# Weight block sums of a seven-product matrix scheme: from VectorE subtractions to adding transfers

## The chip, the cores and the metric

The kernel runs on one core of a Trainium2 chip. A core has five engines that run side by side and wait for one another through semaphores: TensorE (PE: matrix products, with a second stream, PEld, that loads the stationary operand), VectorE (DVE: elementwise work), ScalarE (ACT: functions, copies and casts), GpSimd (POOL) and SyncE (SP, which here only issues transfers). Sixteen transfer (DMA) engines move data between the chip's main memory and the core's on-chip memory; transfers can be issued from SP's queue, from ACT's or from GpSimd's. PE writes its products into eight banks of a separate accumulation memory.

The metric is the device time of one execution, in microseconds (us), the median of several runs. A profile is one further execution, recorded by the hardware.

## The reference

A decoder of two layers over 512 tokens of width 1024. Each layer is a feed-forward block, a mixing block (three kinds of attention with gates), and a second feed-forward block, each between two RMS norms. All values are float32. The change touches the four feed-forward blocks alone:

```python
D_MODEL, SEQ, DEPTH = 1024, 512, 2
D_FF = 2816                       # 22 tiles of 128

def _swiglu(t, w_gate, w_up, w_down):
    return (jax.nn.silu(t @ w_gate) * (t @ w_up)) @ w_down
...
for l in range(DEPTH):
    f = _swiglu(_rmsnorm(h, ffn1_pre_g[l]), ffn1_w_gate[l], ffn1_w_up[l], ffn1_w_down[l])
    h = h + 0.5 * _rmsnorm(f, ffn1_post_g[l])
    ...
    f = _swiglu(_rmsnorm(h, ffn2_pre_g[l]), ffn2_w_gate[l], ffn2_w_up[l], ffn2_w_down[l])
    h = h + 0.5 * _rmsnorm(f, ffn2_post_g[l])
```

## The kernel before

**Precision.** Every operand of a product is split into a high part (a cast to the format that PE multiplies) and a low part (the rest). A product is then three matmuls (`mm3`, L214 to L216): high by high, high by low, low by high. `split` (L185) makes the two parts: a cast on ACT (L188, or L191 with a scale) and a subtraction on DVE (L189 or L192).

**Seven products instead of eight.** The feed-forward's matrix products are cut into 2 x 2 blocks and computed with seven block products, numbered 0 to 6, in the manner of Strassen and Winograd. Four of the products need sums or differences of weight blocks, and four need sums of blocks of the other factor. One *set* of seven block products is one run through the scheme. Each feed-forward block has six sets: four *column groups* of the gate and up projection (`group`, with `gate_up` as the product; tile names with `t`, as in `pta`, `raw_ta`, `kta`, `wh_ta`), whose left block column is the gate weight and whose right block column is the up weight, and two halves of the down projection (`products`, with `product`; names with `d`, as in `pda`, `raw_da`, `bta`). The letter at the end, a or c, is the first or the second feed-forward block of a layer. The rest of the hidden width goes through ordinary products (`halved`, `gates`, `ups`, `down`), which lie between the sets.

**Units.** A block of weights has four tiles of 128 rows and is loaded as two *units* of two tiles (128 x 1024 elements, 512 KB). `BlockUnit` (L288 on) is such a unit. Its `fetch` issues transfers: into a raw buffer (tag `raw`, a ring of four buffers) or into a *kept* tile (`Keep`, L358; `kt` tiles of the tag `v` in a column group, `bt` tiles of the tag `k` in a down half). Its `load` forms the block that the product needs and splits it into `wh` and `wl` (four buffers each). With (row, column) for a block of the weights, the raw transfers and sums were:

- product 0: block (0,0), raw; product 1: block (1,0), raw
- product 2: t = (0,1) - (0,0): the first into kept tile 0, the second raw; one subtraction (L337)
- product 3: t = (1,1) - t: (1,1) into kept tile 1; one subtraction (L340)
- product 4: (1,1) from kept tile 1
- product 5: (1,1) - (0,1): the second raw; one subtraction in place (L345)
- product 6: t with (1,0), raw; one subtraction in place (L349)

The column groups run the products in the order 0, 2, 3, 4, 5, 1, 6 (`ORDER`), but the first group of a block in the order 0 to 6 (`FIRST`); the down halves run in `ORDER`.

**Order of the work.** `Queue` holds a list of jobs, each with the units it needs. When a job begins, its own units are loaded and then those of the jobs after it until four units are ahead (`load_ahead`, `AHEAD = 4`). After each load `fetch_ahead` walks along the list and fetches what isn't fetched yet; it stops at the first unit that needs a ring buffer when all four are taken. A compiler behind this text assigns the buffers and all semaphores and orders each engine's instructions by priority and estimated times, except where `tc.keep_in_program_order` pins one to its place in the text (the transfers into kept tiles are pinned). All weight transfers before the change are issued by SP (L262, L313). GpSimd has some small work at the beginning and in the mixing blocks (L123, L124: two small vector loads that PE transposes at L127; L1174, L1445 to L1447, L1249 to L1251) and none in the feed-forward sets.

Of the kernel before, what the change touches and what calls it, by code (L numbers as in the profile page):

```python
# [12 lines left out]
AF = mybir.ActivationFunctionType  # L13
ALU = mybir.AluOpType
# [3 lines left out]
P = 128  # L18
# [4 lines left out]
def kernel(  # L23
# [38 lines left out]
    nc = tc.nc  # L62
# [225 lines left out]
    class BlockUnit(Unit):  # L288
# [4 lines left out]

        BLOCKS = ((0, 0), (1, 0), (0, 0), None, None, (0, 1), (1, 0))

        def __init__(self, n, src, rows, k0, nk, ncol, keep, name, pair=None):
# [3 lines left out]
            self.pair = pair  # L302

        def waits(self):
            return not self.fetched

        def ring(self):
            return self.BLOCKS[self.n] is not None

        def block(self, dst, b):  # L310
            r = (b[0] * self.rows + self.k0) * P
            src, c = (self.src, b[1] * self.ncol) if self.pair is None else (self.pair[b[1]], self.c0)
            return nc.sync.dma_start(dst, src[r:r + self.nk * P, c:c + self.ncol].rearrange("(k p) c -> p k c", p=P))  # L313

        def fetch(self):
            if self.fetched:
                return
            self.fetched = True
            if self.n == 2:
                tc.keep_in_program_order(self.block(self.keep.get(0, self.k0), (0, 1)))  # L320
            if self.n == 3:
                tc.keep_in_program_order(self.block(self.keep.get(1, self.k0), (1, 1)))
            if self.ring():
                Q.fetched += 1
                self.raw = stile([P, self.nk, self.ncol], "raw", "raw_" + self.name, F32)
                self.block(self.raw[:], self.BLOCKS[self.n])

        def load(self):
            if self.h is not None:
                return  # L330
            self.fetch()
            t = self.keep.get(0, self.k0) if self.n >= 2 else None
            b = self.keep.get(1, self.k0) if self.n >= 3 else None
            if self.n < 2:
                src = self.raw[:]
            elif self.n == 2:
                nc.vector.tensor_tensor(t, t, self.raw[:], ALU.subtract)  # L337
                src = t
            elif self.n == 3:
                nc.vector.tensor_tensor(t, b, t, ALU.subtract)  # L340
                src = t
            elif self.n == 4:
                src = b
            elif self.n == 5:
                nc.vector.tensor_tensor(b, b, self.raw[:], ALU.subtract)  # L345
                src = b
            else:
                ins = (t, self.raw[:]) if self.pair is None else (self.raw[:], t)
                nc.vector.tensor_tensor(t, *ins, ALU.subtract)  # L349
                src = t  # L350
            self.split_from(src)
            if self.ring():
                self.raw = None
                Q.fetched -= 1
            Q.fetch_ahead()
# [288 lines left out]
    def ffn(l, src, wg, wu, wd, dst, name, spare, aside=None):  # L644
# [45 lines left out]
        def parts_of(n):  # L690
            r, tag = st["a", n]
            t = stile([P, 2, 4, S // 2], tag, f"ag{name}_{n}")
            split(t[:, 0], t[:, 1], r)
            st["ag", n] = t

        def sums():

            whole(1, 0)
            whole(1, 1)
            block_sum(2, 11, 10, 11, ALU.add, "k")  # L700
# [4 lines left out]
            block_sum(3, 0, 11, 0, ALU.subtract, "k")  # L705
            parts_of(3)
            yield
            whole(0, 1)
            block_sum(4, 1, 1, 0, ALU.subtract, "tri")
            parts_of(4)  # L710
            parts_of(5)
            yield
# [17 lines left out]
        def gate_up(f, n, uns, last_of_top):  # L730
            seeded = ("gb", 1) in st if n == 1 else False
            if n in (0, 1, 2) and not seeded:
                st["gb", SUM[n]] = [pbank("mm", f"pt{name}_{f}_{n}_{e}") for e in range(2)]
            pts = st.pop(("gb", 1)) if n == 1 else st["gb", SUM[n]]
            opens, ends = n in (0, 1, 2), n in (1, 4, 6)
            for un in uns:
                for k in range(un.nk):
                    kk = un.k0 + k
                    for e in range(2):
                        mm3(pts[e][:], *input_block(n, kk, e), un.h[:, k], un.l[:, k], opens and kk == 0 and not seeded,  # L740
                            ends and kk == ND // 2 - 1, free=True)
# [12 lines left out]
            if n == 1 and not seeded:  # L754
                nc.scalar.activation(t[:], t[:], AF.Silu)
            if n == 4 and last_of_top == 1:
                st["gb", 1] = seeds("mm", f"pt{name}_{f}_1", [st["c", 0, 0][:, e] for e in range(2)])
            if n == 6 or n == last_of_top:
                u = st["c", i, 1]
                nc.vector.tensor_tensor(u[:], u[:], st["c", i, 0][:], ALU.mult)  # L760
                st["hid", f, i] = u

        def feature_major(f):

            for i in range(2):
                u = st.pop(("hid", f, i))
                for b in range(2):
# [7 lines left out]
                    out_ = pt[:].rearrange("p (m q) -> p m q", m=2)  # L775
                    nc.scalar.copy(pair(f2)[:, :, HALVES[i]], out_)

        def group(f):

            order = FIRST if f == TG[0] else ORDER  # L780
            top = max((1, 4), key=order.index)
            keep = Keep(lambda i, k0: stile([P, 2, S], "v", f"kt{name}_{f}_{i}_{k0}", F32)[:])
            for n in order:
                uns = []
                for k in range(0, ND // 2, 2):
                    uns.append(BlockUnit(n, wg[l], ND // 2, k, 2, S, keep, f"t{name}_{f}_{n}_{k}", (wg[l], wu[l])))
                    uns[-1].c0 = f * P
# [56 lines left out]
        def first_factor(ci, n):  # L844

            nm = f"{name}_{ci}_{n}"
            h, l = (stile([P, FC // 2, S // 2], "v", f"a{x}{nm}")[:] for x in "hl")
            if n == 2:
                st["s", ci] = stile([P, FC // 2, S // 2], "v", f"as{nm}", F32)[:]
            for b in range(2):  # L850
                a = lambda i, j: hr[FC // 2 * ci + 2 * j + b][:, :, HALVES[i]]
                two = slice(2 * b, 2 * b + 2)
                s = st["s", ci][:, two] if ("s", ci) in st else None
                if n == 2:
                    nc.vector.tensor_tensor(s, a(1, 0), a(1, 1), ALU.add)
                elif n == 3:
                    nc.vector.tensor_tensor(s, s, a(0, 0), ALU.subtract)
                elif n == 4:
                    nc.vector.tensor_tensor(s, a(0, 1), s, ALU.subtract)
# [3 lines left out]
                split(h[:, two], l[:, two], from_, scale=-1.0 if n == 6 else None)  # L863
            st["a", ci, n] = h, l


# [32 lines left out]
        def products(ci):  # L899
# [7 lines left out]
            for n in ORDER:  # L907
                uns = [BlockUnit(n, w, FC // 2, k, 2, S, keep, f"d{name}_{ci}_{n}_{k}") for k in range(0, FC // 2, 2)]
                yield uns, (lambda n=n, uns=uns: product(ci, n, uns))

        marks, todo = {}, iter(())
# [74 lines left out]
    def down(w, ktiles, act, emit, name, dst, marks, before=None, carry=False):  # L986
# [780 lines left out]
```

## Time and profile before

| | |
|---|---|
| median of 3 runs | 2374.71 us (2374.66 to 2377.28) |
| the profiled execution | 2375.59 us |
| its span, first to last instruction | 2373.9 us |
| granted clock of PE, mean | 0.999 |
| instructions | 31,089 |
| matrix instructions on PE | 11,688 |
| moved by transfers | 349.73 MB, 147 GB/s over the span |

A page of the profile has, in this order: the busy time of each engine and its share of the span; the span in 40 slices; the transfer queues; the chain of work that ended last (for every step, what released it); the costliest groups of instructions; and the transfers by their source and target. A group row reads: line, engine, operation, target<-sources by the program's names, shape, count | busy time in us, mean ns of one | idle time of the engine just before them and what ended it. Matmuls overlap: the row of one gives the time from its start to the modelled end of its results, and the next starts before that. A line in the list of waits reads: engine, its instruction and line <- what it waited for: us in total, times, longest.

### The profile page before, as it was taken

The page shows a single profiled execution, that of the slowest core. Times are in us where ns is not written, and L with a number is a line of the kernel's source. Part 1 is how long each engine was busy: PE and PEld are TensorE (multiplying, and loading weights), DVE is VectorE, ACT ScalarE, POOL GpSimd, SP SyncE. Part 2 cuts the span into 40 slices and gives each one's busy share as a digit, 9 for nine tenths or more (in the row PEclk, how much of TensorE's full clock was granted, in tenths as well). Part 3 has the DMA queues.
Part 4 walks back from the last instruction along what each step waited for, and adds up shares of the span by engine and source line. Part 5 has one row for each costly group of instructions (what it writes and reads, how often), then busy time and mean ns, then how long its engine had stood idle before and what let it go on. Part 6 is the DMA issues. An engine that isn't in the chain of part 4 may idle for free.

```text
span 2373.9 us, 31089 instructions
## 1 busy us (share of the span) xinstructions
PE 2362.5 (100%) x11688; PEld 1997.1 (84%) x11688; DVE 1868.3 (79%) x2532; ACT 1412.3 (59%) x2292; POOL 73.9 (3%) x130
## 2 busy tenths in 40 slices
PE   9999999999999999999999999999999999999998
PEld 8888888888888898888888888888888888888887
DVE  8888977778776688889787789766787766877895
ACT  5766555677665555565655665656675655556654
POOL 1000000001110000000000000000001100000000
PEclk9999999999999999999999999999999999999999
DMA  6555565222323445645646455632232244464553
GB/s 213 192 181 169 170 236 144 72 72 80 88 64 118 157 159 165 218 143 165 233 142 210 149 184 195 208 104 80 63 90 80 72 139 145 160 199 157 178 169 133
DMA packets 232603, 349.73 MB, mean 147 GB/s; under 512 B 10730, under 2 KB 117506, under 8 KB 231940
## 3 DMA queue, kind: packets, MB, share of 16 engines
q1 hardware_dynamic: 232352, 347.71, 45.9%
q8 instruction: 92, 1.51, 0.3%
q14 instruction: 59, 0.48, 0.1%
q0 software_dynamic: 96, 0.03, 0.0%
q10 hardware_dynamic: 4, 0.00, 0.0%
HBM read 333.02 MB, written 14.68 MB: 146 GB/s over the span
## 4 chain that ended last, share of the span: by engine, by line
PE 97%; DVE 2%; ACT 1%; DMA 0%; issue 0%; DVEq 0%; SPq 0%; ACTq 0%
PE pta L215 4%; PE pta L214 4%; PE pta L216 4%; PE ptc L214 4%; PE ptc L215 4%; PE ptc L216 4%; PE pg L214 4%; PE pg L216 4%; PE pg L215 4%; PE pdc L216 3%; PE pdc L214 3%; PE pdc L215 3%; PE pda L216 3%; PE pda L215 3%; PE pda L214 3%; PE pb L214 2%
## 5 line engine op out<-in xcount | busy, mean ns | idle before, releaser
L214 PE MATMUL pg<-us_a,wh_wg 128*128 128x512 f32 x384 | 151.0, 393 | 0.0
L216 PE MATMUL pg<-us_a,wl_wg 128*128 128x512 f32 x384 | 149.7, 390 | 0.0
L215 PE MATMUL pg<-us_a,wh_wg 128*128 128x512 f32 x384 | 149.6, 390 | 0.0
L188 ACT CAST wh_tc<-ktc 128x1024 fp32r<-128x1024 f32 x80 | 84.3, 1054 | 64.3 <-PE ptc L216 34.5
L188 ACT CAST wh_ta<-kta 128x1024 fp32r<-128x1024 f32 x80 | 84.2, 1053 | 55.6 <-PE pta L216 30.4
L189 DVE TENSOR_TENSOR wl_tc<-ktc,wh_tc 128x1024 fp32r<-128x1024 f32 x80 | 97.7, 1222 | 23.4 <-ACT wh_tc L188 23.2
L189 DVE TENSOR_TENSOR wl_ta<-kta,wh_ta 128x1024 fp32r<-128x1024 f32 x80 | 97.6, 1221 | 21.7 <-ACT wh_ta L188 21.5
L214 PE MATMUL pta<-wh_ta,aga 128*128 128x512 f32 x256 | 100.3, 392 | 0.1
L214 PE MATMUL ptc<-wh_tc,agc 128*128 128x512 f32 x256 | 100.3, 392 | 0.0
L215 PE MATMUL pta<-wl_ta,aga 128*128 128x512 f32 x256 | 99.7, 390 | 0.4 <-DVE wl_ta L189 0.4
L215 PE MATMUL ptc<-wl_tc,agc 128*128 128x512 f32 x256 | 99.7, 389 | 0.0
L216 PE MATMUL ptc<-wh_tc,agc 128*128 128x512 f32 x256 | 99.3, 389 | 0.0
L216 PE MATMUL pta<-wh_ta,aga 128*128 128x512 f32 x256 | 99.3, 389 | 0.0
L216 PE MATMUL pda<-wh_da,ala 128*128 128x512 f32 x224 | 87.4, 390 | 0.2 <-DVE ala L189 0.2
L216 PE MATMUL pdc<-wh_dc,alc 128*128 128x512 f32 x224 | 87.4, 390 | 0.0
L214 PE MATMUL pdc<-wh_dc,ahc 128*128 128x512 f32 x224 | 87.4, 390 | 0.0
L214 PE MATMUL pda<-wh_da,aha 128*128 128x512 f32 x224 | 87.3, 390 | 0.0
L215 PE MATMUL pda<-wl_da,aha 128*128 128x512 f32 x224 | 87.2, 389 | 0.0
L215 PE MATMUL pdc<-wl_dc,ahc 128*128 128x512 f32 x224 | 87.2, 389 | 0.0
L216 PEld LDWEIGHTS pg<-us_a,wl_wg 128*128 128x128 f32 x384 | 72.1, 188 | 15.3
L215 PEld LDWEIGHTS pg<-us_a,wh_wg 128*128 128x128 f32 x384 | 72.2, 188 | 14.1
L214 PEld LDWEIGHTS pg<-us_a,wh_wg 128*128 128x128 f32 x384 | 72.1, 188 | 14.1
(543 smaller groups left out, 7515.6 us busy)
## 6 DMA issues: line engine op xcount, KB each, us to landing
raw_ta<-in_ffn_w_gate_dram SPq DMA_DIRECT2D x64, 512.0 KB, 3.9
raw_tc<-in_ffn_w_gate_dram SPq DMA_DIRECT2D x64, 512.0 KB, 3.9
raw_da<-in_ffn_w_down_dram SPq DMA_DIRECT2D x58, 512.0 KB, 3.8
raw_dc<-in_ffn_w_down_dram SPq DMA_DIRECT2D x58, 512.0 KB, 3.7
raw_wg<-in_w_gate_dram SPq DMA_DIRECT2D x48, 512.0 KB, 3.7
kta<-in_ffn_w_up_dram SPq DMA_DIRECT2D x32, 512.0 KB, 6.1
ktc<-in_ffn_w_up_dram SPq DMA_DIRECT2D x32, 512.0 KB, 5.6
raw_wo<-in_w_out_dram SPq DMA_DIRECT2D x24, 512.0 KB, 3.4
```

What stands on the lines that cost most here:

```text
L188: both = [nc.scalar.copy(h_ap, src)]
L189: make = lambda: nc.vector.tensor_tensor(l_ap, src, h_ap.bitcast(F32), ALU.subtract)
L214: nc.tensor.matmul(pt, lh, rh, start=start, stop=False, skip_group_check=free)
L215: nc.tensor.matmul(pt, lh, rl, start=False, stop=False, skip_group_check=free)
L216: nc.tensor.matmul(pt, ll, rh, start=False, stop=stop, skip_group_check=free)
```

## The change

The products are numbered as before, and their weight blocks have other signs. Products 2 and 5 now need the sum of two raw blocks, (0,1) + (0,0) and (1,1) + (0,1). SP copies the first block into the kept tile, and GpSimd then issues a transfer that adds the second one to it (`accum_op=ALU.add`); no DVE operation is left for them. Products 3 and 6 add a raw block to kept tile 0 in place, on DVE. Product 4 needs block (1,1) alone and uses product 3's raw buffer (its `twin`); product 6 uses product 1's raw buffer in the same way where product 1 comes just before it, in `ORDER`; in `FIRST` it loads its own. A raw buffer that is lent to a twin goes back to the ring only when the twin has been split. Kept tile 1 is now the sum for product 5.

A sum's two transfers are put into the text once another unit has been split (`behind`): in a block's first group product 0 (for 2) and product 3 (for 5) of the same set, after that product 4 (for 2) and product 5 (for 5) of the set before it; and the list's order holds too (a raw unit earlier in the list that finds no ring buffer stops the walk).

The signs that the sums no longer have are made up for elsewhere: in the sums and casts of the other factor (a scale of -1 for product 3), in one elementwise product per column group (scale -1), and in the copies that seed accumulation banks in the last part of the block (scale -1 for the right half).

```diff
-        BLOCKS = ((0, 0), (1, 0), (0, 0), None, None, (0, 1), (1, 0))
+        BLOCKS = {0: (0, 0), 3: (1, 1), 1: (1, 0), 6: (1, 0)}
+        SUMS = {2: (0, (0, 1), (0, 0)), 5: (1, (1, 1), (0, 1))}
...
+            self.pair, self.behind, self.twin = pair, behind, twin
+            self.lent = False
+            if twin is not None:
+                twin.lent = True

         def waits(self):
-            return not self.fetched
+            return not self.fetched and (self.behind is None or self.behind.h is not None)

         def ring(self):
-            return self.BLOCKS[self.n] is not None
+            return self.n in self.BLOCKS and self.twin is None

-        def block(self, dst, b):
+        def block(self, dst, b, **how):
...
-            return nc.sync.dma_start(dst, src[r:r + self.nk * P, c:c + self.ncol].rearrange("(k p) c -> p k c", p=P))
+            issue = nc.gpsimd if how else nc.sync
+            return issue.dma_start(dst, src[r:r + self.nk * P, c:c + self.ncol].rearrange("(k p) c -> p k c", p=P), **how)

         def fetch(self):
...
-            if self.n == 2:
-                tc.keep_in_program_order(self.block(self.keep.get(0, self.k0), (0, 1)))
-            if self.n == 3:
-                tc.keep_in_program_order(self.block(self.keep.get(1, self.k0), (1, 1)))
+            if self.n in self.SUMS:
+                i, one, two = self.SUMS[self.n]
+                t = self.keep.get(i, self.k0)
+                tc.keep_in_program_order(self.block(t, one))
+                tc.keep_in_program_order(self.block(t, two, accum_op=ALU.add))
...
         def load(self):
...
-            elif self.n == 2:
-                nc.vector.tensor_tensor(t, t, self.raw[:], ALU.subtract)
...
-            elif self.n == 5:
-                nc.vector.tensor_tensor(b, b, self.raw[:], ALU.subtract)
...
+            if self.twin is not None:
+                self.raw = self.twin.raw
+            if self.n in self.SUMS:
+                src = self.keep.get(self.SUMS[self.n][0], self.k0)
+            elif self.n in (3, 6):
+                src = self.keep.get(0, self.k0)
+                nc.vector.tensor_tensor(src, src, self.raw[:], ALU.add)
+            else:
+                src = self.raw[:]
             self.split_from(src)
-            if self.ring():
+            if self.raw is not None and not self.lent:
                 self.raw = None
                 Q.fetched -= 1
             Q.fetch_ahead()
...
-            split(t[:, 0], t[:, 1], r)
+            split(t[:, 0], t[:, 1], r, scale=-1.0 if n == 3 else None)
...
-                nc.vector.tensor_tensor(u[:], u[:], st["c", i, 0][:], ALU.mult)
+                nc.vector.scalar_tensor_tensor(u[:], u[:], -1.0, st["c", i, 0][:], ALU.mult, ALU.mult)
...
+        def block_units(order, keep, rows, nm, src, pair=None, c0=0):
+
+            before, made = st.get("units"), {}
+            st["units"] = made
+            for n in order:
+                for k in range(0, rows, 2):
+                    behind, twin = None, None
+                    if n in (2, 5):
+                        behind = made[n // 2 * 2 - 2 + n // 5, k] if before is None else before[4 if n == 2 else 5, k]
+                    if n == 4 or n == 6 and order.index(1) == 5:
+                        twin = made[n - 1 if n == 4 else 1, k]
+                    made[n, k] = BlockUnit(n, src, rows, k, 2, S, keep, f"{nm}_{n}_{k}", pair, behind, twin)
+                    made[n, k].c0 = c0
+                yield n, [made[n, k] for k in range(0, rows, 2)]
...
-                nc.scalar.copy(pt[:, c], dst.fs[t][:, HF[b]][:, c])
+                nc.scalar.activation(pt[:, c], dst.fs[t][:, HF[b]][:, c], AF.Copy, scale=-1.0 if b else 1.0)
```

More of the change, by code (lines that the diff above doesn't have):

```diff
@@ L699, in sums @@
             whole(1, 1)
-            block_sum(2, 11, 10, 11, ALU.add, "k")
+            block_sum(2, 11, 11, 10, ALU.subtract, "k")
             parts_of(2)
@@ L704, in sums @@
             block_sum(5, 10, 0, 10, ALU.subtract, "tri")
-            block_sum(3, 0, 11, 0, ALU.subtract, "k")
+            block_sum(3, 0, 11, 0, ALU.add, "k")
             parts_of(3)
@@ L708, in sums @@
             whole(0, 1)
[L709 removed]
+            block_sum(4, 1, 0, 1, ALU.subtract, "tri")
             parts_of(4)
@@ L782, in group @@
             keep = Keep(lambda i, k0: stile([P, 2, S], "v", f"kt{name}_{f}_{i}_{k0}", F32)[:])
[L783 to L787, printed above, removed]
+            for n, uns in block_units(order, keep, ND // 2, f"t{name}_{f}", wg[l], (wg[l], wu[l]), f * P):
                 yield uns, (lambda n=n, uns=uns: gate_up(f, n, uns, top))
@@ L862, in first_factor @@
                 from_ = a(*((0, 0), (0, 1), None, None, None, None, (1, 1))[n]) if n in (0, 1, 6) else s
-                split(h[:, two], l[:, two], from_, scale=-1.0 if n == 6 else None)
+                split(h[:, two], l[:, two], from_, scale=-1.0 if n == 3 else None)
             st["a", ci, n] = h, l
@@ L906, in products @@
             keep, w = Keep(make), wd[l, ci * FC * P:(ci + 1) * FC * P]
-            for n in ORDER:
-                uns = [BlockUnit(n, w, FC // 2, k, 2, S, keep, f"d{name}_{ci}_{n}_{k}") for k in range(0, FC // 2, 2)]
+            for n, uns in block_units(ORDER, keep, FC // 2, f"d{name}_{ci}", w):
                 yield uns, (lambda n=n, uns=uns: product(ci, n, uns))
```

23 lines of the change are left out of this document (4 added, 19 removed).

## The prediction

> **What bounds the kernel now.** I read the page first, for the engine that is never free.
>
> ```profile
> span 2373.9 us, 31089 instructions
> ...
> PE 2362.5 (100%) x11688; PEld 1997.1 (84%) x11688; DVE 1868.3 (79%) x2532; ACT 1412.3 (59%) x2292; POOL 73.9 (3%) x130
> ...
> q1 hardware_dynamic: 232352, 347.71, 45.9%
> ...
> PE 97%; DVE 2%; ACT 1%; DMA 0%; issue 0%; DVEq 0%; SPq 0%; ACTq 0%
> ```
>
> The chain of waits is matrix products for 97% of the span. How much could be won at all is read from the busy time by stretch (start and length, then PE, PEld, DVE, ACT, POOL, clock, share of the 16 transfer engines, GB/s) and from PE's own waits.
>
> ```profile
> 0.00:20.00 20.00, 18.07 (x87) 12.52 (x88) 12.25 (x27) 13.78 (x24) 2.64 (x10) 1.00 0.94 314
> 20.00:2360.00 2340.00, 2337.12 (x11556) 1977.99 (x11555) 1850.17 (x2491) 1395.87 (x2259) 71.28 (x120) 1.00 0.46 146
> ```
>
> ```profile
> PE ptc L215 <- DVE wl_tc L189: 0.5, 1, 0.5
> PE pga L818 <- ACT us_x L191: 0.4, 1, 0.4
> PE pta L215 <- DVE wl_ta L189: 0.4, 1, 0.4
> ```
>
> From 20 to 2360 us PE is idle for 2340.00 - 2337.12 = 2.9 us; the rest of its idle time is the opening and the closing, which the change doesn't reach. Waits for a weight half amount to 0.5 + 0.4 = 0.9 us. A matmul takes 0.39 us but the next begins after 0.23, so a short wait can hide in the overlap; the timeline shows the pace inside a group:
>
> ```profile
> 62.98 0.39 PE L215 MATMUL pta<-wl_ta,aga 128*128 128x512 f32 x1
> 63.20 0.39 PE L216 MATMUL pta<-wh_ta,aga 128*128 128x512 f32 x1
> 63.43 0.39 PE L214 MATMUL pta<-wh_ta,aga 128*128 128x512 f32 x1
> 63.66 0.39 PE L215 MATMUL pta<-wl_ta,aga 128*128 128x512 f32 x1
> ```
>
> That is (63.66 - 62.98) / 3 = 0.227 us per matmul. One set of seven products is 7 x 4 x 2 x 3 = 168 of them: 38.1 us. A whole set of the third column group:
>
> ```profile
> 141.20:179.40 38.20, 38.20 (x171) 31.59 (x170) 30.64 (x30) 22.52 (x31) 0.00 (x0) 1.00 0.61 193
> ```
>
> 38.2 us, so a set runs at the pace of the matmuls with nothing lost, while DVE works 30.6 us of it. The change adds and removes no matmul. Time can be lost here, hardly won.
>
> **The change part by part.** There are 24 sets (four FFNs, each with four column groups and two halves of the down product), with two units to a product.
>
> *Subtractions removed.* Before, a unit of product 2, 3, 5 and 6 costs one DVE operation each:
>
> ```profile
> L345 DVE TENSOR_TENSOR kta<-kta,raw_ta 128x1024 f32<-128x1024 f32 x16 | 19.6, 1225 | 0.5
> ...
> L337 DVE TENSOR_TENSOR kta<-kta,raw_ta 128x1024 f32<-128x1024 f32 x16 | 19.5, 1220 | 8.0 <-DMA raw_ta<-in_ffn_w_gate_dram 8.0
> ...
> L349 DVE TENSOR_TENSOR kta<-raw_ta,kta 128x1024 f32<-128x1024 f32 x16 | 19.5, 1224 | 8.1 <-DMA raw_ta<-in_ffn_w_gate_dram 8.0
> ...
> L340 DVE TENSOR_TENSOR kta<-kta,kta 128x1024 f32<-128x1024 f32 x16 | 19.4, 1220 | 0.2
> ```
>
> Products 2 and 5 lose theirs (L337, L345); 3 and 6 keep one addition in place. That is 24 x 4 = 96 operations of 1.22 us, 117 us of DVE. All of it lay beside PE: 30.6 falls to 30.6 - 4 x 1.22 = 25.7 us a set, still hidden by 38.2 us of matmuls. On the path it is worth between 0 and 2.9 us (all idle time of the middle); I take 0.9, the two waits for a weight half, the only ones that a less loaded DVE directly ends.
>
> *Signs.* They move into casts and seeds that exist already: a cast with a scale costs what a plain one does (1059 against 1054 ns below). Count it as 0; ACT's free 15.7 us of a set covers it.
>
> ```profile
> L191 ACT ACTIVATE wh_wg<-raw_wg 128x1024 fp32r<-128x1024 f32 x48 | 50.6, 1059 | 14.9 <-PE pg L215 5.8 <-PE pb L215 4.6 <-PE pv L216 3.3
> ...
> L188 ACT CAST wh_ta<-raw_ta 128x1024 fp32r<-128x1024 f32 x32 | 33.5, 1053 | 25.1 <-PE pta L216 15.0 <-issue 6.4 <-PE pga L215 1.9
> ```
>
> *Transfers.* Before, a set loads 14 blocks of 512 KB (ten raw, four kept). After, six raw and eight for the sums, again 14; the first group's order has no twin for product 6 and loads 16, that is 8 more in the kernel. Four of a set's 14 become adding transfers issued by GpSimd: 96 in all. The trace has no adding transfer. The nearest rows (name, count, size, us to landing):
>
> ```profile
> raw_ta<-in_ffn_w_gate_dram SPq DMA_DIRECT2D x64, 512.0 KB, 3.9
> ...
> kta<-in_ffn_w_up_dram SPq DMA_DIRECT2D x32, 512.0 KB, 6.1
> ...
> hsave<-ha SPq DMA_DIRECT2D x8, 512.0 KB, 4.1
> ...
> vecs<-in_b_gate_dram POOLq DMA_DIRECT2D x1, 24.0 KB, 2.8
> ...
> vecs<-in_mem_norm_g_dram POOLq DMA_DIRECT2D x1, 4.0 KB, 1.7
> ```
>
> A plain one occupies 0.61 x 38.2 / 14 = 1.66 us of all 16 engines. An adding one must fetch the block and also read the tile and write it back. Lower bound: a plain load, 1.66 us and 3.9 to landing. Upper bound: load and store twice over, 6.6 us and 2 x (3.9 + 4.1) = 16 us. I take load plus store once, 3.3 us and 8.0 to landing, since that is the data which it must move. The engines then carry 10 x 1.66 + 4 x 3.3 = 29.8 us of 38.2, a share of 0.78, and keep up.
>
> The Trainium skill, "Collectives: The Full Stack", section "The bandwidth ceiling: the fold count and why AG ≠ RS ≠ AR", says that a reducing transfer runs at half the rate of a copy because it has two source reads, not because the add costs time (62.28 against 32.35 GB/s). No row here shows it; by it the share would be (10 + 4 x 1.93) x 1.66 / 38.2 = 0.77, and the sum the same.
>
> *When a sum is due.* Four buffers of wh and wl let a unit be split when the unit four before it has left PE (the casts' wait above is for PE). A unit is 12 matmuls, 2.73 us, so its split starts about 8.2 us before PE needs it and takes 1.05 + 1.22, leaving 5.9 us. In the repeated order a sum is requested when the set before has split product 4 (for 2) or, once the ring passes, product 6 (for 5): nine units, 24.5 us, ahead of its own split. The copy takes 6.1 and the add 8.0: 14.1 against 24.5. In a first group the request comes only four units ahead: 10.9 + 5.9 = 16.8 against 14.1, covered by 2.7 us; at the upper bound it would be 22.1, late by 5.3. The first group of the first FFN has the trace's own margin:
>
> ```profile
> 37.54 0.46 SPq L313 DMA_DIRECT2D kta<-in_ffn_w_up_dram  x1
> ```
>
> ```profile
> 46.23 1.21 DVE L337 TENSOR_TENSOR kta<-kta,raw_ta 128x1024 f32<-128x1024 f32 x1
> ```
>
> ```profile
> 52.79 1.05 ACT L188 CAST wh_ta<-kta 128x1024 fp32r<-128x1024 f32 x1
> ```
>
> The copy leaves SP at 37.54 and the cast comes at 52.79, 15.3 us later: 14.1 fits. If it didn't, the cast would hold ACT's evictions behind it, and then PE for want of a bank.
>
> *Queues.* SP issues 96 transfers fewer and no longer waits as here:
>
> ```profile
> SPq L313 <- DVE kta L345: 108.2, 16, 17.0
> ```
>
> A new wait stands on SP in the second down half: the kept tile has two buffers, so its copy waits until product 5 of the first half is split, two units (5.5 us). Behind it the next raw block is asked for only at product 6's split, so nothing needed is held. The ring of four now holds the shared blocks through two or more products, but a raw block is still requested six splits, 16.4 us, ahead and takes 3.9. On GpSimd each adding issue waits for the copy to land. Queued behind it are other adding issues and, in the first FFN, the small vectors that PE transposes:
>
> ```profile
> 35.13 0.58 POOL L123 DMA_DIRECT2D vecs<-in_mem_norm_g_dram  x1 [3.85 <-DVE sel L158]
> 35.71 0.55 POOL L124 DMA_DIRECT2D vecs<-in_b_gate_dram  x1
> ```
>
> ```profile
> 60.68 0.22 PE L127 MATMUL vecs_t<-ident,vecs 8*128 8x8 f32 x1
> ```
>
> They have 25 us to spare. What GpSimd spends on one adding issue is bounded by 0.55 us (no growth with size) and 0.55 x 8 = 4.4 us (48 rows read and written there, against 256 rows read twice and written here). I take 0.7, near the lower end, because 24 KB costs no more than 4 KB. Four issues are 2.8 us of a set on an idle engine.
>
> *Sum.* 2373.9 of span plus 1.7 around it is the profiled execution's 2375.6 us; less 0.9, plus nothing, is 2374.7. That execution lies 0.9 above the median of the runs, 2374.7; so 2373.8, rounded to **2374 us**.
>
> **The rivals.** A difference of 0.2% (4.7 us) is about what a measurement of this kernel can tell from no change.
>
> *The first groups' sums come late* (slower). It decides from an add that lands after 16.8 - 6.1 = 10.7 us. Halfway to the bound, 13.4, each of 2 sums in 4 FFNs is late by 2.7: 21 us, **2396**. For it: DVE and the engines are fullest at the first FFN's opening. Against: SP can issue ahead of the split that precedes it in the text. Chance 0.20.
>
> *The transfer engines fill up* (slower). From (38.2 - 16.6) / 4 = 5.4 us for an adding transfer, 3.3 times a plain one, a set waits for its weights. At 6.0 a set takes 40.6: 24 x 2.4 = 58 us, **2432**. Against: nothing here is slower than 0.61 without it. Chance 0.10.
>
> *DVE is held while GpSimd writes a transfer's list* (slower). DVE has (38.2 - 25.7) / 4 = 3.1 us to give per adding issue; at 3.75 it costs 24 x 4 x 0.65 = 62 us, **2436**. Chance 0.07. The Trainium skill, "SBUF — State Buffer", section "Who interferes with whom", has that lock between the two engines, but says that a tensor_tensor from SBUF meets only GpSimd's reads. The trace has no GpSimd work inside a set to show it.
>
> *The order doesn't come out as meant* (slower): adding issues placed so that the vectors or a sum stand behind a copy that is itself late, say 10 us once: **2385**. Chance 0.05.
>
> *Faster.* PE's 2.9 us go, and with them as much again that hides in the overlap: **2369**. Chance 0.06.
>
> **How the numbers follow.** No change has 0.52, with its own range 2370 to 2379. Slower is 0.20 + 0.10 + 0.07 + 0.05 = 0.42, faster 0.06. The range 2370 to 2410 leaves out the two fullest cases (0.17) and a little of the faster one.
>
> **What would show it.** Right: DVE near 1750 us, some 96 operations fewer; PE idle for about 3 us between 20 and 2360; the transfer engines' share near 0.78 in a set; adding transfers landing in about 8 us. Wrong: casts of kt tiles or the additions at product 3 that wait for a transfer, with PE waits behind them in a first group (the sums late); sets longer than 38.2 us everywhere (engines or DVE full); DVE operations well above 1.22 us (the lock).

## The result and the profile after

The changed kernel takes 2379.18 us (median of 20 runs, 2377.84 to 2381.62) against 2375.80 us for the kernel before in the same comparison: a ratio of 1.0015, interval 1.0008 to 1.0022. It is 3.4 us slower. The profiled execution took 2378.61 us. Its page (span; busy us and instructions by engine; then two queues with packets, MB and share of the 16 transfer engines):

```profile
span 2376.9 us, 31030 instructions
...
PE 2361.9 (99%) x11688; PEld 1996.9 (84%) x11688; DVE 1764.8 (74%) x2436; ACT 1410.3 (59%) x2291; POOL 189.2 (8%) x226
...
q1 hardware_dynamic: 208416, 301.57, 39.0%
q0 software_dynamic: 26208, 50.37, 12.4%
```

DVE has lost exactly 96 operations and 103.5 us. (Neighbouring DVE operations overlap a little, so this is less than 96 x 1.22.) PE's work is the old one, and the span is 3.0 us longer. Next, busy time by stretch of the changed kernel: the middle, and a set of the third column group (start and length, PE, PEld, DVE, ACT, POOL, clock, transfer share, GB/s).

```profile
20.00:2360.00 2340.00, 2334.55 (x11536) 1975.41 (x11535) 1743.64 (x2392) 1390.80 (x2250) 186.50 (x216) 1.00 0.52 148
144.90:183.10 38.20, 38.20 (x171) 31.59 (x170) 27.23 (x26) 22.53 (x31) 4.79 (x4) 1.00 0.72 192
```

A set in the steady state still takes 38.2 us without a gap, with the transfer engines at 0.72. The loss is therefore not spread over the sets. But PE now idles 2340.00 - 2334.55 = 5.5 us in the middle, where it had idled 2.9. PE's waits (total us, times, longest) name the place, a wait that the kernel before did not have:

```profile
PE pta L214 <- ACT ca L745: 3.5, 2, 3.0
```

The timeline of PE in the changed kernel (start, length, operation) shows it, in the first FFN, in the second column group:

```profile
92.12 0.39 PE L216 MATMUL pta<-wh_ta,us_x 128*128 128x512 f32 x1
95.55 0.50 PE L214 MATMUL pta<-wh_ta,aga 128*128 128x512 f32 x1 [3.04 <-ACT ca L745]
...
97.58 0.63 PE L215 MATMUL pta<-wl_ta,aga 128*128 128x512 f32 x1
98.00 0.63 PE L216 MATMUL pta<-wh_ta,aga 128*128 128x512 f32 x1
98.43 0.63 PE L214 MATMUL pta<-wh_ta,aga 128*128 128x512 f32 x1
98.86 0.63 PE L215 MATMUL pta<-wl_ta,aga 128*128 128x512 f32 x1
```

Product 2 of the second group wants an accumulation bank that product 6 of the first group still holds. ACT is to empty it (L745, the Silu). After the wait the matmuls start (98.86 - 97.58) / 3 = 0.427 us apart for a while instead of 0.227, so the wait costs more than its 3.5 us. In the kernel before, PE goes from product 0 to product 2 there without a stop, with this matmul:

```profile
94.00 0.39 PE L214 MATMUL pta<-wh_ta,aga 128*128 128x512 f32 x1
```

Why the eviction is late is read from ACT's timeline. First the changed kernel, then the kernel before, both in the same stretch:

```profile
83.28 1.06 ACT L1087 ACTIVATE mst<-mst 128x1024 f32<-128x1024 f32 x1 [3.84 <-DMA mst<-in_mem_dram]
...
91.87 0.20 ACT L1089 ACTIVATE mem_rstd<-mem_rstd 128x1 f32<-128x1 f32 x1
92.09 1.28 ACT L1090 ACT_TABLE_LOAD   x1
93.39 0.20 ACT L1090 ACTIVATE mem_rstd<-mem_rstd 128x1 f32<-128x1 f32 x1
93.61 1.28 ACT L745 ACT_TABLE_LOAD   x1
94.90 0.60 ACT L745 ACTIVATE ca<-pta 128x512 f32<-128x512 f32 x1
```

```profile
82.03 1.06 ACT L1081 ACTIVATE mst<-mst 128x1024 f32<-128x1024 f32 x1 [0.80 <-DMA mst<-in_mem_dram]
...
91.13 0.20 ACT L1083 ACTIVATE mem_rstd<-mem_rstd 128x1 f32<-128x1 f32 x1
91.35 1.28 ACT L749 ACT_TABLE_LOAD   x1
92.64 0.60 ACT L749 ACTIVATE ca<-pta 128x512 f32<-128x512 f32 x1
...
94.69 1.28 ACT L1084 ACT_TABLE_LOAD   x1
95.98 0.20 ACT L1084 ACTIVATE mem_rstd<-mem_rstd 128x1 f32<-128x1 f32 x1
```

In this stretch ACT also computes the statistics of the memory (`mem_stats`): for each of two 512 KB blocks a Square, an Ln and an Exp, and each change of function loads a table for 1.28 us. The eviction stands behind part of that chain. Two things moved. The first Square starts at 83.28 instead of 82.03, since its block landed later (although it was asked for 1.8 us earlier). And the second Exp with its table, 1.5 us, now stands ahead of the eviction instead of behind it. Both versions have the same list of instructions here; only their order on ACT differs. The eviction starts at 94.90 instead of 92.64, 2.26 us later, while PE ends product 0 of the second group 1.6 us earlier than before. Before, the first bank came free 0.8 us ahead of PE (92.64 + 0.60 against 94.00), and the second just in time.

The memory blocks land later because the transfers beside them are heavier; here that is a reading of the rows, and run 7 tests it. The first block is asked for at 75.28 and read at 83.28 in the changed kernel, at 77.12 and 82.03 in the kernel before: 8.0 us against 4.9. The view of the issues has a time to landing (shortest, median, longest) for one of the two blocks only, in the changed kernel the first, and then in the kernel before the second:

```profile
DMA to landing us min/median/max: 7.9/7.9/7.9
```

```profile
DMA to landing us min/median/max: 5.5/5.5/5.5
```

The stretches from 80 to 100 us, of the changed kernel and then of the kernel before, have the transfer share in the last column but one:

```profile
80.00:90.00 10.00, 10.00 (x45) 8.02 (x44) 4.34 (x7) 6.67 (x11) 1.20 (x1) 1.00 1.10 269
90.00:100.00 10.00, 6.50 (x22) 4.67 (x21) 6.11 (x14) 8.74 (x13) 0.00 (x0) 0.84 0.35 90
```

```profile
80.00:90.00 10.00, 10.00 (x45) 8.00 (x44) 6.85 (x11) 8.55 (x14) 0.00 (x0) 1.00 0.74 243
90.00:100.00 10.00, 10.00 (x47) 8.06 (x46) 7.48 (x13) 9.93 (x14) 0.00 (x0) 1.00 0.00 0
```

The share is 1.10 against 0.74, and work runs on into the next stretch. (A share above 1 means that packets in flight overlap.) In the last stretch PE is busy 6.50 us against 10.00.

### The profile page after: what moved, and what is told of

It reads as the page before. It is cut to its first block, busy times and chain, and to the rows that moved or that the text cites. A ratio compares the mean times of both kernels' runs of the same rounds, so it can differ in the third digit from the quotient of the medians.

```text
span 2376.9 us, 31030 instructions
## 1 busy us (share of the span) xinstructions
PE 2361.9 (99%) x11688; PEld 1996.9 (84%) x11688; DVE 1764.8 (74%) x2436; ACT 1410.3 (59%) x2291; POOL 189.2 (8%) x226
## 3 DMA queue, kind: packets, MB, share of 16 engines
q0 software_dynamic: 26208, 50.37, 12.4%
## 4 chain that ended last, share of the span: by engine, by line
PE 96%; DVE 1%; ACT 1%; DMA 1%; issue 0%; DVEq 0%; ACTq 0%
PE ptc L214 4%; PE ptc L216 4%; PE ptc L215 4%; PE pta L214 4%; PE pta L215 4%; PE pta L216 4%; PE pg L214 4%; PE pg L216 4%; PE pg L215 4%; PE pdc L216 3%; PE pda L216 3%; PE pdc L214 3%; PE pda L215 3%; PE pdc L215 3%; PE pda L214 3%; PE pb L214 2%
## 5 line engine op out<-in xcount | busy, mean ns | idle before, releaser
L189 DVE TENSOR_TENSOR wl_tc<-ktc,wh_tc 128x1024 fp32r<-128x1024 f32 x64 | 78.3, 1223 | 54.4 <-ACT wh_tc L188 54.4
L189 DVE TENSOR_TENSOR wl_ta<-kta,wh_ta 128x1024 fp32r<-128x1024 f32 x64 | 78.3, 1223 | 51.4 <-ACT wh_ta L188 51.3
L188 ACT CAST wh_tc<-ktc 128x1024 fp32r<-128x1024 f32 x64 | 67.5, 1055 | 53.5 <-PE ptc L216 36.5
L188 ACT CAST wh_ta<-kta 128x1024 fp32r<-128x1024 f32 x64 | 67.4, 1054 | 51.1 <-PE pta L216 35.5
L189 DVE TENSOR_TENSOR wl_tc<-raw_tc,wh_tc 128x1024 fp32r<-128x1024 f32 x48 | 58.6, 1223 | 35.2 <-ACT wh_tc L188 34.8
L215 PEld LDWEIGHTS pg<-us_a,wh_wg 128*128 128x128 f32 x384 | 72.2, 188 | 14.1
```

The source lines that it names most:

```text
L188: both = [nc.scalar.copy(h_ap, src)]
L189: make = lambda: nc.vector.tensor_tensor(l_ap, src, h_ap.bitcast(F32), ALU.subtract)
L215: nc.tensor.matmul(pt, lh, rl, start=False, stop=False, skip_group_check=free)
```

## The experiments

Theory A: the loss is this one eviction, late by the memory blocks' landing and by ACT's order; the removed subtractions bring a small gain that it outweighs. The rivals are in the expectations. Each ratio is to the kernel before, run on the same chip in the same comparison.

**1 and 2. The statistics taken out, of both kernels.**

```diff
 def mem_stats():
-    (loads of the memory blocks, Square, Ln, Exp and DVE's steps)
+    memset of mem_rstd to 1
```

> The changed kernel with the statistics of mem (two loads, squares, and a Ln/Exp chain on ACT in the first FFN) left out: their result is set to 1. Theory A (the whole loss is one PE stall at 92 to 100 us of the first FFN, where the eviction of product 6 stands behind that chain on ACT; apart from it the change saves 1 to 2 us): the stall of 3.2 us and the small ones behind it are gone, 2373 to 2375 us, ratio to before 0.9990 to 0.9997. Theory B (adding transfers cost a little everywhere, the stall is only where it shows): 2377 to 2379, ratio about 1.001.

> The kernel before with the same statistics left out. It shows no stall at that place, so A and B both expect no gain of more than 0.5 us: 2375 to 2376. What tells them apart is the pair: by A e1 is 1 to 2 us below this one, by B it is 2 to 3 us above.

Measured: after without statistics 2374.00 us, 0.9991 (0.9983 to 1.0000), and no wait for L745; before without statistics 2375.59, 0.9997 (0.9988 to 1.0007). With the chain gone from both, loads and steps on ACT, the changed kernel is 1.6 us below the other. The loss needs the chain; the sums, which stayed, bring none without it.

**3. The statistics kept in program order.** Nothing is left out. `keep_in_program_order` holds an instruction at its place in the program's order, and the plan can't move it.

```diff
-nc.scalar.activation(ss[:, 1:2], ss[:, 1:2], AF.Exp, scale=-0.5)
+tc.keep_in_program_order(nc.scalar.activation(ss[:, 1:2], ss[:, 1:2], AF.Exp, scale=-0.5))
 (the same for every ACT and DVE operation of mem_stats)
```

> The changed kernel with the chain kept at its place in the text, so that both evictions of product 6 come before its Ln and Exp on ACT; loads and work are the same. Theory A1 (the order on ACT makes the stall: one more Exp and its table load ahead of the eviction): stall gone, 2374 to 2375.5. Theory A2 (the loads of mem land late because the transfer engines are full, and ACT waits for them): ACT still waits for the first load at 83 us, a stall of 1 us or more stays at 92 to 96 us, 2376 to 2378.

Measured: 2373.24 us, 0.9991 (0.9982 to 1.0000). ACT's timeline in this kernel:

```profile
84.92 1.06 ACT L1087 ACTIVATE mst<-mst 128x1024 f32<-128x1024 f32 x1 [1.87 <-DMA mst<-in_mem_dram]
...
87.61 0.60 ACT L745 ACTIVATE ca<-pta 128x512 f32<-128x512 f32 x1 [0.60 <-PE pta L216]
...
89.25 0.58 ACT L745 ACTIVATE ca<-pta 128x512 f32<-128x512 f32 x1
...
91.67 1.28 ACT L1089 ACT_TABLE_LOAD   x1
```

The blocks still land late, even later than in the changed kernel (the Square starts at 84.92), but the evictions come at 87.61 and 89.25, ahead of every table load, and PE doesn't wait. Another order alone removes the loss. This version is 5.9 us below the changed kernel's median, and the two ratios' intervals don't meet. Against the kernel before it is at the edge of what could be told.

**4. Less to load in the first group.** There, too, product 6 takes the raw block of product 1 in place of a second load.

```diff
-if n == 4 or n == 6 and order.index(1) == 5:
+if n in (4, 6):
```

> The changed kernel with product 6 sharing product 1's raw buffer in the first groups too: two 512 KB loads fewer in each first group, order on ACT the same. A1: the stall at 92 us shrinks by no more than the lateness of the loads, 0.8 to 1.3 us: 2377.5 to 2378.5. A2: mem lands in 5 to 6 us instead of 7.9 and the stall is nearly gone: 2374.5 to 2376. If the shared buffers starve the ring, new waits of ACT or DVE for raw loads show in the first groups and the time rises over 2380.

Measured: 2380.97 us, 1.0023 (1.0014 to 1.0032), so the expected relief failed. There are two transfers fewer, but the adding ones moved. One now follows 0.2 us behind the first memory block instead of 2.9; that block is read 9.4 us after its issue instead of 8.0, and the wait grew. PE's wait in this kernel:

```profile
PE pta L214 <- ACT ca L745: 4.4, 1, 4.4
```

The first group shows something else: here the prediction's rival of the late sums comes true. The adds for product 5 are issued at 49.96 and 53.50 instead of 58.61 and 59.99, right behind those for product 2, which then land in 8.6 us instead of 5.9 to 6.1. ACT's casts of product 2 wait for them, 1.8 and 1.1 us, and soon after PE waits 1.1 us for a weight half. The first of these casts and that matmul:

```profile
53.34 1.05 ACT L188 CAST wh_ta<-kta 128x1024 fp32r<-128x1024 f32 x1 [1.77 <-DMA kta<-in_ffn_w_gate_dram]
```

```profile
60.68 0.49 PE L215 MATMUL pta<-wl_ta,aga 128*128 128x512 f32 x1 [1.14 <-DVE wl_ta L189]
```

**5. Control for 3: the kernel before, pinned in the same way** (the same edit).

> The kernel before, with the memory statistics' ACT and DVE operations kept in program order, as in the pinned version of the changed kernel. Theory A (the changed kernel loses by the eviction that stands behind the late statistics; the kernel before had no such stall): nothing to cure here, 2374.8 to 2376.2 us, ratio to before 0.9995 to 1.0005, and the pinned changed kernel (2373.24 us) lies 1.5 to 2.5 us below it, which is what the removed subtractions are worth. Rival B (this order is better in any kernel, and the changed kernel's gain is the order's alone): 2373.0 to 2373.6 us, like the pinned changed kernel.

Measured: 2376.41 us, 1.0004 (0.9995 to 1.0013). Pinning gains nothing there, which speaks against rival B. But it isn't a clean control: the pinned DVE operations brought a wait of 1.7 us of their own, for a DVE addition at L753. Run 11 repeats it without that.

**6. The statistics later**, in the first FFN's down product.

```diff
-    Q.add([], lambda: iter(mem_stats() or ()))     (among the column groups)
 ...
+    if name == "a0":
+        Q.add([], lambda: iter(mem_stats() or ())) (in the down product)
```

> The changed kernel with the job of the memory statistics moved from the first FFN's column groups to its down product; nothing left out. Theory A: between the first two sets of the first FFN no eviction stands behind a Square, Ln or Exp any more, PE doesn't wait for L745, and the time is that of the pinned version, 2372.8 to 2374.2 us. Rival B (the transfers are full in the first 100 us in any case, so a sum or a weight is late there as soon as the memory loads no longer are): PE waits of 1 us or more for a weight half in the first groups, 2375 to 2378 us. Rival C (the statistics chain meets another eviction later): a wait of 1 to 3 us in the down product, 2376 to 2379 us.

Measured: 2388.22 us, 1.0053 (1.0040 to 1.0065): rival C, and dearer than it said. PE's wait, then ACT's timeline in this kernel:

```profile
PE pda L214 <- ACT aha L188: 9.8, 2, 7.2
```

```profile
254.61 1.06 ACT L1088 ACTIVATE mst<-mst 128x1024 f32<-128x1024 f32 x1 [3.55 <-DMA mst<-in_mem_dram]
...
264.57 0.20 ACT L1090 ACTIVATE mem_rstd<-mem_rstd 128x1 f32<-128x1 f32 x1
264.68 0.60 ACT L188 CAST aha<-hra 128x512 fp32r<-128x512 f32 x1
```

The wait at L745 is gone, and the casts of the next product's activations stand behind the same chain instead. The chain is what costs, wherever something urgent follows it on ACT.

**7. GpSimd's transfers without the add.** GpSimd still issues them. The order of instructions on every engine is the changed kernel's.

```diff
-issue = nc.gpsimd if how else nc.sync
+issue, how = (nc.gpsimd if how else nc.sync), {}
 ...
-tc.keep_in_program_order(self.block(t, two, accum_op=ALU.add))
+tc.keep_in_program_order(self.block(t, two, plain=True))
```

> The changed kernel with GpSimd's adding transfers turned into plain ones of the same size, places and issues (the sums are left out: products 2 and 5 use one raw block); the order of instructions on every engine is that of the changed kernel. It measures what the adding costs, and parts the late landing of the memory blocks from the order on ACT. Price, by the prediction (an adding transfer is a load and a store, twice a plain one): the software queue's share falls from 12.4% to 6.2 to 7%, landing from 6.5 to 9 us to 4 to 5 us. If the adding cost no more than a plain load, both stay. Theory A (lateness 1.25 us by the memory blocks and 1.0 us by the order): the memory blocks land 0.8 to 1.3 us earlier, the wait for L745 shrinks to 1 to 2.3 us, 2376.5 to 2378.2 us. Rival B (the order alone): the wait stays at 3 us, 2378.5 to 2379.5 us. Rival C (the full transfers alone): no wait for L745, 2373 to 2375 us.

Measured: 2375.83 us, 0.9999 (0.9990 to 1.0008), a little better than theory A's range. PE's wait in this kernel, its queue of GpSimd's transfers, one issue group on POOL, and the memory blocks' time to landing:

```profile
PE pta L214 <- ACT ca L745: 1.2, 2, 0.7
```

```profile
q0 software_dynamic: 13920, 50.37, 6.6%
```

```profile
L318 POOL DMA_DIRECT2D kta<-in_ffn_w_up_dram x16 | 11.6, 728 | 86.6 <-DMA kta<-in_ffn_w_up_dram 40.3 <-DVE ala L189 22.4 <-PE pta L216 11.0
```

```profile
DMA to landing us min/median/max: 5.6/5.6/5.6
```

With ACT's order unchanged and the blocks even earlier than in the kernel before (the first Square starts at 81.23), 1.2 us of the wait's 3.5 remain. The eviction comes at 92.85, only 0.2 us later than in the kernel before, but PE is 1.4 us ahead of that kernel here, so a gain elsewhere has used up the slack. For the price of the add see the points below.

**8. The removed DVE work put back on the sums**, on top of run 3's edit.

```diff
 if self.n in self.SUMS:
     src = self.keep.get(self.SUMS[self.n][0], self.k0)
+    nc.vector.tensor_tensor(src, src, src, ALU.max)
```

> The pinned changed kernel with one DVE operation of the old kind and size put back into each of the 96 units of products 2 and 5 (the maximum of the sum with itself, which changes nothing). Theory A (the removed subtractions ended waits for weight halves): DVE back at 1860 to 1890 us, PE again waits 0.5 to 1.5 us for weight halves between 20 and 2360 us, and the time is 0.8 to 2 us above the pinned version, 2374.0 to 2375.2 us. Rival B (DVE's work is hidden by the matmuls; the gain is from elsewhere, the earlier loads or the order): 2373.0 to 2373.6 us.

Measured: 2531.03 us, 1.0653 (1.0638 to 1.0668), far outside both expectations. It doesn't measure DVE's work. DVE's waits, and its timeline around one of them:

```profile
DVE kta L341 <- DMA kta<-in_ffn_w_gate_dram: 47.4, 8, 9.3
```

```profile
197.99 1.23 DVE L341 TENSOR_TENSOR kta<-kta 128x1024 f32<-128x1024 f32 x1 [6.92 <-DMA kta<-in_ffn_w_up_dram]
199.13 1.22 DVE L189 TENSOR_TENSOR wl_ta<-raw_ta,wh_ta 128x1024 fp32r<-128x1024 f32 x1
```

The added operation stands in DVE's queue ahead of a split whose raw block is there, and waits up to 9 us for an adding transfer; the split waits with it, and PE for the split. It is the same mechanism as on ACT, and it spreads over the sets: DVE's waits for adding transfers at L341 add up to 222 us, in column groups and down halves alike.

**9. The same DVE work, on raw blocks of products 0 and 4**, on top of run 3's edit.

```diff
-    src = self.raw[:]
+    src = self.raw[:]; [nc.vector.tensor_tensor(src, src, src, ALU.max) for _ in range(self.n in (0, 4))]
```

> The pinned changed kernel with one DVE operation of the old size (the maximum of a block with itself, which changes nothing) in each of the 96 units of products 0 and 4, on raw blocks that SP's queue loads, so that no DVE operation waits for an adding transfer. It puts back the amount of DVE work that the change removed. Theory A (the removed work ended short waits for weight halves, and that is the gain of the pinned version): DVE 1860 to 1890 us, PE again waits 0.5 to 2 us for weight halves, 2374.0 to 2375.6 us. Rival B (DVE's amount of work is hidden, the gain is from elsewhere): 2372.8 to 2373.6 us. If it is far above 2380 us, then what costs is any DVE operation put before a cast, and not, as in the run before, that it waits for an adding transfer.

Measured: 2375.18 us, 1.0001 (0.9992 to 1.0009), DVE 1865.3 us. PE's wait in this kernel, then the stretch from 60 to 70 us, of this kernel and of the kernel before:

```profile
PE pta L215 <- DVE wl_ta L189: 0.5, 1, 0.5
```

```profile
60.00:70.00 10.00, 9.47 (x42) 7.55 (x41) 9.34 (x10) 5.28 (x6) 2.49 (x2) 1.00 0.82 165
```

```profile
60.00:70.00 10.00, 9.61 (x41) 7.67 (x42) 9.43 (x9) 5.95 (x7) 0.00 (x0) 1.00 0.40 117
```

PE's wait for a weight half is back, in the stretch where the kernel before had lost 0.39 us and the changed and the pinned kernel lost nothing. By the ratios the DVE work put back costs 0.0010, or 2.4 us, with overlapping intervals. That is too much for the removed work: about 1.1 us of it arises at 25 us, where the added operations of product 0 stand ahead of DVE's L604 and PE waits for that, and the kernel before has neither. And run 8's loss does come from the wait for adding transfers: the same number of DVE operations elsewhere costs nearly nothing.

**10. Only ACT's order undone.** Square, Ln and Exp are pinned, DVE's steps are free.

```diff
-nc.scalar.activation(ss[:, 1:2], ss[:, 0:1], AF.Ln)
+tc.keep_in_program_order(nc.scalar.activation(ss[:, 1:2], ss[:, 0:1], AF.Ln))
 (the same for Square and Exp)
```

> The changed kernel with the Square, Ln and Exp of the memory statistics alone kept in program order on ACT (DVE's are left free). The second Ln and Exp then stand behind the eviction L745 as in the kernel before, and the memory blocks land as late as in the changed kernel. Theory A (late blocks and order each cost a part): the wait for L745 is 0.5 to 2 us, and the time 2374.2 to 2376.5 us, between the pinned version and the changed kernel. Rival B (the order alone): no wait, 2373 to 2374 us. Rival C (the late blocks alone): the wait stays at 3 us, 2377.5 to 2379.5 us.

Measured: 2373.89 us, 0.9996 (0.9987 to 1.0005). ACT's timeline in this kernel, and its stretch from 90 to 100 us:

```profile
84.30 1.06 ACT L1087 ACTIVATE mst<-mst 128x1024 f32<-128x1024 f32 x1 [1.24 <-DMA mst<-in_mem_dram]
...
92.71 1.09 ACT L745 ACTIVATE ca<-pta 128x512 f32<-128x512 f32 x2
93.81 1.28 ACT L1089 ACT_TABLE_LOAD   x1
```

```profile
90.00:100.00 10.00, 9.88 (x49) 7.96 (x48) 7.81 (x12) 9.91 (x15) 0.00 (x0) 1.00 0.44 104
```

The blocks are as late as in the changed kernel (8.2 us to landing), and PE loses only 0.12 us: the time lies in rival B's range, below theory A's. But this order is better than the old one. Here the second Ln stands behind the eviction too, and in the kernel before it stood ahead of it (91.13). With that Ln and its table, 1.5 us, put back, the eviction would come at 94.2 and PE would wait some 1.5 us, by estimate. So the new order alone leaves 1.2 us of waiting (run 7; with the second Exp behind it the eviction would come 1.5 us earlier there and PE would not wait, by estimate), both together 3.5, and a good enough order absorbs the lateness whole (run 10). What late blocks would cost with exactly the old order wasn't tried.

**11. Control for 10: the kernel before, pinned in the same way.**

> The kernel before with the Square, Ln and Exp of the memory statistics alone kept in program order on ACT: a control for the pinned version that leaves DVE's order freer than the first control, which had got a wait of 1.7 us for a DVE addition of its own. Theory A (the pinned changed kernel gains by the removed DVE work): 2375.0 to 2376.4 us, 1.5 to 3 us above the pinned changed kernel. Rival B (it gains by the order): 2373.0 to 2374.0 us.

Measured: 2374.61 us, 1.0002 (0.9993 to 1.0011), against 2374.64 for the kernel before in that comparison. The time is below the range that theory A had given, but the ratio shows no gain, and rival B's lay lower still. It still has PE's wait of 0.4 us for a weight half.

## Why the prediction was wrong, point by point

The forecast was 2374 us, no change; the result is slower by more than the comparison's uncertainty. That the time lies inside the stated range is luck: the case that came isn't among those that drew it. None of its signs of being wrong came either; of its signs of being right one failed, PE's idle time in the middle (5.5 us for about 3).

*Subtractions removed: right in sign, the size partly by luck.* 0.9 us was forecast, for two waits for a weight half. Both are gone in the changed kernel, but only the one at 61 us goes with the subtractions: every version of the kernel before keeps it, and PE is 0.7 us further ahead after it. The one of 0.5 us at `ptc` is missing in runs 2, 5 and 11 too, where nothing was taken from DVE's sums (and another, at the output weights, of 0.3 to 0.9 us, comes and goes in versions of both kernels). Each pair of kernels with the statistics treated alike shows a gain: ratios lower by 0.0006 (1 against 2), 0.0006 (10 against 11) and 0.0013 (3 against 5, where 5 has a wait of its own), so 1.4 us in the two clean pairs (by their medians 1.6 and 0.7). Their intervals overlap; the sign is supported three times, the size only roughly.

*Signs: right.* Nothing in the waits names a cast or a seed with a scale.

*Price of an adding transfer: right in size.* 3.3 us of 16 engines was forecast; 12.4% of 2376.9 us over 96 transfers is 3.07, and without the add 6.6% of 2374.2 is 1.63. So the add costs 1.88 plain transfers. The Trainium skill, "Collectives: The Full Stack", section "The bandwidth ceiling: the fold count and why AG ≠ RS ≠ AR", has a measured ratio of 1.93 between a copying and a reducing collective; this case's 1.88 is close to it. To landing, 8.0 us was forecast; the changed kernel's issues (name, count, size, median us to landing) show 6.1 to 9.0, but those issued between 72 and 83 us, around the memory blocks, took 9.5 to 12.8:

```profile
kta<-in_ffn_w_up_dram POOLq DMA_DIRECT2D x16, 512.0 KB, 9.0
...
btc<-in_ffn_w_down_dram POOLq DMA_DIRECT2D x16, 512.0 KB, 6.1
```

*GpSimd's issue: off in size, without effect.* 0.7 us was taken; one takes 1.2 on the idle engine. The 0.7 is what a plain one of the same size costs (728 ns in run 7).

```profile
L318 POOL DMA_DIRECT2D kta<-in_ffn_w_up_dram x16 | 19.3, 1204 | 84.0 <-PE pta L216 24.9 <-DMA kta<-in_ffn_w_up_dram 23.5 <-DVE wl_ta L189 15.0
```

*When a sum is due: right, but closer than it reads.* In the changed kernel no cast and no addition holds PE for want of a sum, in the first groups either. The rival with the largest chance, first sums late, didn't come: in the first group of the first FFN the adds landed in 5.9 to 8.8 us, under its 10.7, and the casts came 1.4 to 2.9 us after them. Run 4 shows how little it takes. For product 2 of the second group, copy and add took 18 us (64.03 to 82.1) where 14.1 was forecast; the cast came at 88.00, and that margin of 24.0 us was forecast well (24.5). Nor did full engines come in the steady sets (0.72 where 0.78 was forecast), or DVE held by GpSimd (1.22 us for an addition).

*Queues: the step that failed, and with it the "plus nothing" of the sum.* It read "Queued behind it are other adding issues and, in the first FFN, the small vectors that PE transposes", and the share of the engines was worked out for a steady set alone. It asked who waits in a queue for a weight or a vector, and not which other loads share the engines in the first 100 us, nor what is computed from them. The two memory blocks do, and on ACT their statistics stand ahead of an eviction that had no slack. The rival "The order doesn't come out as meant" named the kind of mishap, but on GpSimd's and SP's queues and not on ACT, and as a small case. The runs showed instead: in place of nothing the eviction behind the late statistics costs 5.3 us, 3.5 of it waiting. With ACT's new order alone 1.2 us of waiting are left (7), the fuller engines' late blocks raise it to 3.5, and with the side job behind the eviction next to nothing is lost (3, 10).

The sum of the profiled executions closes. Set side by side matmul by matmul, the changed kernel is 0.7 us ahead by the end of the opening. There the four `gqx` matmuls, from the same start at 3.99, took 2.26 us against 3.78. So they did in the profiled executions of runs 4, 7 and 8, and not in those of the other five versions of the changed kernel; why stays open. It wins 0.7 more at 61 us (the weight half) and 0.2 by 83, then loses 5.3 between 92 and 100 us, which is 3.5 of waiting and 1.8 of slow matmuls, wins back 0.6 later and ends 3.0 behind.

Why the planned order puts the second Exp ahead of the eviction in the changed kernel wasn't tried: the order on every engine is laid down before the kernel runs, and no run here shows by what.

## What to carry to other kernels

An added transfer's price is not only its own landing: list every other load in flight in the same stretch, and follow what is computed from it until that meets an in-order queue with an urgent operation behind it. Where an eviction stands just in time behind a side job with table loads, pin the side job behind the eviction before you judge a change elsewhere; moving it without pinning (run 6) only finds the next victim. The target of an adding transfer is best read first by the operation that needs it, and not by an extra operation that others in the same queue stand behind (run 8).

## What the runs showed of the hardware

A wait of 3.0 us on PE was followed by matmuls 0.427 us apart and a granted clock of 0.84 for the stretch from 90 to 100 us; within it the clock is 0.50 from 97 to 100 us. Waits of 0.7 us or less (runs 7 and 10) left the clock at 1.00. The length of a wait alone doesn't tell: one of 1.7 us (run 5, at 123 us) left it at 1.00 too, while in the changed kernel's opening one of 1.0 us, up to 7.78, was followed by 0.57 from 8 to 12 us. The Trainium skill, "TensorE: Matmul & The Clock Gate", section "Wait — 56ns, not 53.3ns?", gives 426.7 ns from start to start for this size while the array is cold, and this case's 427 agrees.

Each change between Silu, Ln and Exp cost ACT 1.28 us for the table, and the next operation began right after it; five such loads, 6.4 us, lie between the first Square and the eviction in the changed kernel.
